# Blocks of 32 slots for every expert of layer 2, four experts to a one-hot product

## The chip, the cores and the metric

The kernel is one launch on one core of a Trainium2 chip. The metric is the device time of that launch in microseconds (us), as the median of several runs. Beside it stands one profiled execution, whose trace gives the busy time and the waits of each engine: PE (TensorE, with its weight loads as PEld), DVE (VectorE), ACT (ScalarE), POOL (GpSimd) and SP (SyncE, which here only issues DMAs).

## The reference, cut to what matters

Two layers run one after the other. Each ends with a grouped mixture of 16 experts, of which a token uses two (in layer 2 only the 256 latent tokens are left, so 512 pairs of token and expert):

```python
best = jnp.argmax(group_score, axis=-1)              # 1 of 4 groups
_, local = lax.top_k(in_group, TOP_K)                # 2 of its 4 experts
w = ROUTED_SCALE * w / jnp.sum(w, axis=-1, keepdims=True)
...
def expert(acc, ew):
    wg, wu, wd, cw = ew                              # 1024x512, 1024x512, 512x1024, one weight per token
    y = (jax.nn.silu(h @ wg) * (h @ wu)) @ wd
    return acc + cw[:, None] * y, None
...
x_lat = layer_norm(alpha * x_lat + g2 * f_lat, ln2_g[l], ln2_b[l])
```

On the inputs that the reference draws, its router sends to the experts of layer 2, in the order in which the kernel takes them, 37, 31, 10, 27, 68, 41, 14, 18, 82, 41, 14, 21, 19, 39, 30 and 20 tokens. Two of these counts are over 64, and six are over 32.

## The kernel before, in words

The order of the instructions on each engine is written out by hand. In a layer's expert stage the tokens are first gathered by expert into the columns of `XgT` (a product with a one-hot matrix). `ORDER` then names the experts one by one; below, expert q is the one at place q of that order, from 0 to 15. An expert's tokens are worked on in blocks of slots. `blocks` lists the first slot and the number of slots of each. The first block always runs. Each further one stands in a nest of branches (`over`), taken by PE, ACT, DVE and POOL where the expert's count of tokens is larger than the block's first slot; a branch hint is given one step ahead (`foretell`). In layer 2 the blocks were 64 slots, then 32, 32, 64 and 64.

For one block the steps are these.

- `take` (DVE) copies the block's columns from `XgT` into a small tile, `xs` for a first block and `xo` for a further one. The place of the columns is read from a register; an expert that is not the first of its group needs two copies (L1510, L1512).
- `up` (PE, L1533) multiplies the block with the two weight matrices `wg` and `wu`. The block's columns are the stationary operand and the weights stream past it. With 64 slots two products of 512 streamed columns stand side by side in the array for each of the eight parts of the contraction; with 32 slots four products of 256 do.
- `gate` (ACT L1539, DVE L1540) makes the hidden values, `turn` (PE L1547, ACT L1548) transposes them.
- `down` (PE, L1564) multiplies them with `wd`, by the same rule of two or four products side by side, into one PSUM tile, `yp`, that all blocks of layer 2 use in turn.
- DVE takes the result out of PSUM, scaled (L1578), in as many pieces as there are products side by side: into `y` for a first block, into `yo` (named `x` in the rows) for a further one.
- `place_rows` (DVE, L1474 and L1475) makes a one-hot matrix with the routing weights, `S` for first blocks and `So` for further ones, and `scatter` (PE, L1481) adds S-transposed times the outputs to four PSUM tiles `cps`, which hold all 256 tokens and the residual until the end of the layer.

With first blocks of 64 slots, two experts fill the 128 rows of one `y` and one `S`, so that `scatter` runs once for two experts. A further block has a scatter of its own, over its 32 rows alone.

The loop over q interleaves neighbours: three eighths of the `up` of expert q+1, `turn` of q, then (in turn with q) `place_rows` or `scatter` of a pair, then the branch with `down` of q and the further blocks of q, then the other five eighths of `up` of q+1 and its `gate`. The expert weights come in pages of 1 MB, six to an expert, 96 in all, through 16 buffers (`feed`): SP issues the load of a page when the page 16 places ahead of it has been read for the last time, further blocks included.

Of the kernel before, what the change touches and what calls it, by code (L numbers as in the profile page):

```python
# [30 lines left out]
ALU = mybir.AluOpType  # L31
# [64 lines left out]
def _body(ctx, tc, nc, I, out, dbg):  # L96
# [6 lines left out]
    pe, act, dve, pool, sp = nc.tensor, nc.scalar, nc.vector, nc.gpsimd, nc.sync  # L103
# [222 lines left out]
    for l in range(NL):  # L326
        first = l == 0
# [970 lines left out]
        for a in range(T):  # L1298
            dve.tensor_scalar(oh[:, a, :], io[:, :CAP], pos[:, a:a + 1], None, op0=ALU.is_equal)

        blocks = [(0, 64), (64, 32), (96, 32)]
        blocks += [(128, 32), (160, 32)] + [(r, 64) for r in range(192, CAP, 64)] if first else [(128, 64), (192, 64)]
        NB = len(blocks)
        RR = (CAP - M0) // 64
        n4, p4 = n6.rearrange("p (g k) -> p g k", k=6), p6.rearrange("p (g k) -> p g k", k=6)
# [113 lines left out]
        def slot_cols():  # L1419


            wide = [128, NB, 16]
            sl, pc, fl, u = (sc[:, n, :16 * NB].rearrange("p (b e) -> p b e", e=16) for n in range(4))
            sid = cnt[:, 7, 0:2]
            pool.iota(sid[:, 0:1], pattern=[[0, 1]], base=0, channel_multiplier=1,
                      allow_small_or_imprecise_dtypes=True)
            for b, (r0, _) in enumerate(blocks):
                pool.memset(sl[:, b, :], float(r0))
            dve.tensor_scalar(sid[:, 1:2], sid[:, 0:1], 64.0, -64.0, op0=ALU.is_ge, op1=ALU.mult)
            dve.tensor_tensor(sid[:, 0:1], sid[:, 0:1], sid[:, 1:2], op=ALU.add)  # L1430
            dve.tensor_scalar(sl, sl, sid[:, 0:1], None, op0=ALU.add)

            def each(n):
                return cnt[:, n, None, :].to_broadcast(wide)

            dve.tensor_tensor(cnt[:, 4], cnt[:, 3], cnt[:, 2], op=ALU.subtract)
            dve.tensor_tensor(cnt[:, 4], cnt[:, 4], cnt[:, 1], op=ALU.subtract)
            thr = cnt[:, 5].rearrange("p (g e) -> p g e", e=4)
            dve.memset(thr[:, :, 0], 0.0)
            dve.tensor_copy(thr[:, :, 1], nA[:, :, 1])  # L1440
            dve.tensor_tensor(thr[:, :, 2], nA[:, :, 2], n4[:, :, 4], op=ALU.add)
            dve.memset(thr[:, :, 3], 1.0e6)
            dve.tensor_tensor(u, sl, each(1), op=ALU.is_ge)
            dve.tensor_tensor(u, u, each(4), op=ALU.mult)
            dve.tensor_tensor(pc, sl, each(2), op=ALU.add)
            dve.tensor_tensor(pc, pc, u, op=ALU.add)
            dve.tensor_tensor(u, sl, each(0), op=ALU.is_ge)
            dve.scalar_tensor_tensor(pc, u, 1.0e6, pc, op0=ALU.mult, op1=ALU.add)
            dve.tensor_tensor(fl, each(5), sl, op=ALU.is_gt)

            for n, t in ((0, pc), (1, fl)):
                d = sc[:, 3, 80 + 8 * n:88 + 8 * n].rearrange("p (j g) -> p g j", j=4)
                t4 = t[:, 0].rearrange("p (g j) -> p g j", j=4)
                for h in range(2):
                    dve.tensor_copy(d[64 * h:64 * h + 64], t4[64 * h:64 * h + 64, h::2, :])
            return pc, fl, sc[:, 3, 80:88], sc[:, 3, 88:96]

        def token_rows():

# [8 lines left out]
            act.activation(posrow, yp_[0][:, 0:256], AF.Copy)  # L1468
            act.activation(w0row, yp_[0][:, 256:512], AF.Copy)
            act.activation(wdrow, pt_[0][:, 256:512], AF.Copy)  # L1470

        def place_rows(dst, rows, pcol, fcol):

            dve.scalar_tensor_tensor(dst[rows], wdrow[rows], fcol[rows], w0row[rows], op0=ALU.mult, op1=ALU.add)  # L1474
            dve.scalar_tensor_tensor(dst[rows], posrow[rows], pcol[rows], dst[rows], op0=ALU.is_equal, op1=ALU.mult)  # L1475
# [74 lines left out]
        def down(e, b):  # L1550
# [15 lines left out]
            if not first:  # L1566
                q = ORDER.index(e)
                if b == 0:
                    rows = slice(64 * (q % 2), 64 * (q % 2) + 64)
                    yt = [y_[q // 2 % 2][:, 512 * n:512 * n + 512] for n in range(2)]  # L1570
                else:
                    rows, yt = slice(64, 64 + Mb), yo
                if b:
                    place_rows(So, rows, pcol[:, b, e:e + 1], fcol[:, b, e:e + 1])
                for j in range(ng):
                    n, c = divmod(N * j, 512)
                    part = slice(Mb * j, Mb * j + Mb)
                    dve.tensor_tensor(yt[n][rows, c:c + N], yp[part, :N], g2[n][part, c:c + N], op=ALU.mult)  # L1578
                if b:
                    scatter(So, yo, rows)  # L1580
                return
            for j in range(ng):
                src, dst = yp[Mb * j:Mb * j + Mb, :N], y[:, N * j:N * j + N]
# [87 lines left out]
        for q, e in enumerate(ORDER):  # L1671
# [10 lines left out]
            if q == 2 and not first:  # L1682
                for i in tiles:
                    for n in range(2):
                        pe.matmul(cps[i, n], ident, X[i][n], start=False, stop=False, skip_group_check=True)
            if not first and q % 2:
                place_rows(S_[q // 2 % 2], slice(0, 128), pcols[:, q // 2:q // 2 + 1], fcols[:, q // 2:q // 2 + 1])
            elif not first and q:
                scatter(S_[(q // 2 - 1) % 2], [y_[(q // 2 - 1) % 2][:, 512 * n:512 * n + 512] for n in range(2)],
                        slice(0, 128))  # L1690
            if q == 0 and LATE:
                for un in late[1:] if LATE == 1 else late:
                    un.mm(pt_[1][:, 256:])
# [225 lines left out]
```

## Time and profile before

| what | value |
|---|---|
| median of 3 runs | 1500.34 us (1496.33 to 1503.78) |
| the profiled execution, its own time | 1505.39 us |
| its span in the trace | 1503.7 us |
| PE busy | 1334.2 us, 89% of the span |
| DVE busy | 739.6 us, 49% |
| ACT busy | 449.3 us, 30% |
| mean granted TensorE clock | 0.949 of full |
| read from HBM | 342.63 MB |

A share of the span is a mean over stages. The expert stage of layer 2 runs from about 1218 us to 1493 us of the span, and after it only the last normalization and the stores remain, up to 1503.7 us. Layer 1 comes before it and keeps its blocks. The granted clock is given as a share of full speed: 1.00 is 2.4 GHz and 0.50 is 1.2 GHz.

### The profile page before, as it was taken

How to read it: one execution, taken by the hardware profiler on the slowest of the kernel's cores; microseconds unless marked ns; L12 is line 12 of the kernel's file. 1: busy time of each engine (PE TensorE's matmuls, PEld its weight loads, DVE VectorE, ACT ScalarE, POOL GpSimd, SP SyncE). 2: the span in 40 equal slices, each digit the busy share in tenths (PEclk: the TensorE clock that was granted, in tenths of full speed). 3: DMA queues.
4: the chain of work that ended last, by engine and by line, in shares of the span. 5: the costliest groups of instructions: out<-in, count | busy, mean ns of one | idle time of the engine just before them, and what ended most of it. 6: DMA issues, size and time to landing. Idle time of an engine off the chain costs nothing. (4 is left out here: it accounts for less than half of the span.)

```text
span 1503.7 us, 21798 instructions
## 1 busy us (share of the span) xinstructions
PE 1334.2 (89%) x8147; PEld 843.9 (56%) x8147; DVE 739.6 (49%) x1448; ACT 449.3 (30%) x781; POOL 138.2 (9%) x251
## 2 busy tenths in 40 slices
PE   5999889999999978988988779869998889989976
PEld 4777667777787853323333368546767753333322
DVE  3376774553466671323222456887676762222323
ACT  2437533333241221210111173764434320000000
POOL 0020000000022210000000441100002110000000
PEclk9999999999999988998989889999999999898988
DMA  9494332332353377998897646535535579988891
GB/s 377 172 376 173 135 143 89 114 143 85 112 191 118 131 321 300 418 414 346 330 386 280 214 131 231 192 130 200 219 118 205 180 309 403 371 325 340 353 402 49
DMA packets 56816, 358.15 MB, mean 238 GB/s; under 512 B 7316, under 2 KB 8116, under 8 KB 17920
## 3 DMA queue, kind: packets, MB, share of 16 engines
q1 hardware_dynamic: 46048, 320.83, 54.7%
q0 software_dynamic: 9808, 33.39, 6.6%
q8 instruction: 111, 1.82, 0.5%
q10 hardware_dynamic: 720, 1.06, 0.2%
q14 instruction: 129, 1.06, 0.2%
HBM read 342.63 MB, written 12.62 MB: 236 GB/s over the span
## 5 line engine op out<-in xcount | busy, mean ns | idle before, releaser
L373 PE MATMUL acc<-whi,pg 128*128 128x512 f32 (+1 forms) x424 | 173.6, 409 | 0.0
L374 PE MATMUL acc<-wlo,pg 128*128 128x512 f32 (+1 forms) x424 | 165.7, 391 | 4.6 <-DVE wlo L361 4.3
L375 PE MATMUL acc<-whi,pg 128*128 128x512 f32 (+1 forms) x424 | 164.8, 389 | 0.0
L361 DVE TENSOR_TENSOR wlo<-pg,whi 128x1024 fp32r<-128x1024 f32 x104 | 127.0, 1222 | 71.5 <-ACT whi L360 71.2
L360 ACT ACTIVATE whi<-pg 128x1024 fp32r<-128x1024 f32 x104 | 109.5, 1055 | 83.5 <-PE acc L375 54.8
L1564 PE MATMUL sd<-pg,lnv 128*64 128x512 f32 (+1 forms) x416 | 78.0, 566 | 21.2 <-issue 11.0
L374 PEld LDWEIGHTS acc<-wlo,pg 128*128 128x128 f32 x424 | 80.6, 190 | 24.5 <-DVE wlo L361 8.7
L373 PEld LDWEIGHTS acc<-whi,pg 128*128 128x128 f32 x424 | 80.6, 190 | 21.8 <-issue 5.2
L375 PEld LDWEIGHTS acc<-whi,pg 128*128 128x128 f32 x424 | 80.4, 190 | 15.9
L1564 PE MATMUL sd<-pb,lnv 128*64 128x512 f32 (+1 forms) x416 | 70.7, 543 | 14.8 <-ACT lnv L1548 7.1
L1533 PE MATMUL acc<-pg,xs 128*64 128x512 f32 x256 | 71.4, 655 | 13.8 <-DMA pg<-in_wg 4.3
L1539 ACT ACTIVATE hh<-sd 64x512 f32<-64x512 f32 (+1 forms) x18 | 10.2, 568 | 198.7 <-PE sd L1533 198.7
L1533 PE MATMUL acc<-pb,xs 128*64 128x512 f32 x256 | 64.1, 617 | 3.4 <-DMA pb<-in_wu 2.6
L1585 DVE COPY y<-sd 64x512 f32<-64x512 f32 (+1 forms) x32 | 17.9, 558 | 99.6 <-ACT y L1587 83.1
L1533 PE MATMUL sd<-pg,xs 128*64 128x512 f32 x256 | 61.5, 621 | 1.5 <-issue 1.5
L373 PE MATMUL acc<-whi,yhi 128*128 128x512 f32 x144 | 60.3, 419 | 0.0
L1533 PE MATMUL sd<-pb,xs 128*64 128x512 f32 x256 | 59.9, 610 | 0.0
L718 ACT ACTIVATE P<-sd,sm 128x512 f32<-128x512 f32 (+1 forms) x48 | 29.0, 614 | 103.1 <-DVE sm L711 103.1
L1564 PEld LDWEIGHTS sd<-pg,lnv 128*64 128x64 f32 (+1 forms) x416 | 25.4, 135 | 60.3 <-issue 53.9
L375 PE MATMUL acc<-whi,ylo 128*128 128x512 f32 x144 | 57.0, 396 | 0.8 <-DVE ylo L553 0.8
L374 PE MATMUL acc<-wlo,yhi 128*128 128x512 f32 x144 | 56.9, 395 | 0.0
L1533 PEld LDWEIGHTS acc<-pg,xs 128*64 128x64 f32 x256 | 23.3, 149 | 57.6 <-issue 46.0
(470 smaller groups left out, 2378.4 us busy)
## 6 DMA issues: line engine op xcount, KB each, us to landing
pg<-in_win SPq DMA_DIRECT2D x40, 1024.0 KB, 6.0
pg<-in_wada SPq DMA_DIRECT2D x40, 1024.0 KB, 6.2
pg<-in_wg SPq DMA_DIRECT2D x32, 1024.0 KB, 13.6
pg<-in_wu SPq DMA_DIRECT2D x32, 1024.0 KB, 15.5
pb<-in_wd SPq DMA_DIRECT2D x32, 1024.0 KB, 10.0
pb<-in_wg SPq DMA_DIRECT2D x32, 1024.0 KB, 14.3
pb<-in_wu SPq DMA_DIRECT2D x32, 1024.0 KB, 16.4
pg<-in_wd SPq DMA_DIRECT2D x32, 1024.0 KB, 10.3
```

The lines of the kernel that those rows point to most:

```text
L360: act.activation(hi, raw, AF.Copy)
L361: dve.tensor_tensor(lo, raw, hi.bitcast(F), op=ALU.subtract)
L373: pe.matmul(ps, ah, bh, start=start, stop=False)
L374: pe.matmul(ps, ah, bl, start=False, stop=False)
L375: pe.matmul(ps, al, bh, start=False, stop=stop)
L718: act.activation(p[:, s], bank[g][:, s], AF.Exp, scale=SCALE, bias=sm[:, 0, i:i + 1], accum_out=sm[:, 1, i:i + 1])
L1533: pe.matmul(gu[Mb * j:Mb * j + Mb, :N], xv[:, k, 0:Mb], w[k // 4][:, k % 4, c:c + N], start=k == 0, stop=k == 7, skip_group_check=True)
L1539: act.activation(hh[:, :N], gu[0:64, :N], AF.Silu)
L1564: pe.matmul(yp[Mb * j:Mb * j + Mb, :N], lt, wd[f // 2][:, f % 2, N * j:N * j + N], start=f == 0, stop=f == 3, skip_group_check=True)
L1585: dve.tensor_copy(dst, src)
```

## The change

In layer 2 the list of blocks becomes 32, 32, 32, 32, 64 and 64 slots; in layer 1 the new expression gives the same list as the old one. The outputs of four first blocks now share one `y` tile and one one-hot matrix, so `place_rows` for them comes at q = 3, 7, 11, 15 and `scatter` at q = 4, 8, 12 and after the last expert. The scatter of a further block now runs over all 128 rows: `So` and `yo` are set to zero once (POOL), and for a block of 32 the rows 96 to 128 of `So` are cleared again each time (DVE). The columns that hold each slot's place and choice of weight (`slot_cols`) are made for the new layout.

```diff
-        blocks = [(0, 64), (64, 32), (96, 32)]
-        blocks += [(128, 32), (160, 32)] + [(r, 64) for r in range(192, CAP, 64)] if first else [(128, 64), (192, 64)]
+        if first:
+            blocks = [(0, 64)] + [(r, 32) for r in range(64, 192, 32)] + [(r, 64) for r in range(192, CAP, 64)]
+        else:
+            blocks = [(r, 32) for r in range(0, 128, 32)] + [(r, 64) for r in range(128, CAP, 64)]
...
-            dve.tensor_scalar(sl, sl, sid[:, 0:1], None, op0=ALU.add)
+            dve.tensor_scalar(sl[:, 1:], sl[:, 1:], sid[:, 0:1], None, op0=ALU.add)
+            dve.tensor_scalar(sid[:, 1:2], sid[:, 0:1], 32.0, -32.0, op0=ALU.is_ge, op1=ALU.mult)
+            dve.tensor_scalar(sl[:, 0], sl[:, 0], sid[:, 0:1], sid[:, 1:2], op0=ALU.add, op1=ALU.add)
...
-                d = sc[:, 3, 80 + 8 * n:88 + 8 * n].rearrange("p (j g) -> p g j", j=4)
-                t4 = t[:, 0].rearrange("p (g j) -> p g j", j=4)
-                for h in range(2):
-                    dve.tensor_copy(d[64 * h:64 * h + 64], t4[64 * h:64 * h + 64, h::2, :])
+                for g in range(4):
+                    p = slice(32 * g, 32 * g + 32)
+                    dve.tensor_copy(sc[p, 3, 4 * n:4 * n + 4], t[p, 0, 4 * g:4 * g + 4])
...
+            for t in [So] + yo:
+                pool.memset(t, 0.0)
...
-                    rows = slice(64 * (q % 2), 64 * (q % 2) + 64)
-                    yt = [y_[q // 2 % 2][:, 512 * n:512 * n + 512] for n in range(2)]
+                    rows = slice(32 * (q % 4), 32 * (q % 4) + 32)
+                    yt = [y_[q // 4 % 2][:, 512 * n:512 * n + 512] for n in range(2)]
...
+                    if Mb == 32:
+                        dve.memset(So[96:128], 0.0)
...
-                    scatter(So, yo, rows)
+                    scatter(So, yo, slice(0, 128))
...
-            if not first and q % 2:
-                place_rows(S_[q // 2 % 2], slice(0, 128), pcols[:, q // 2:q // 2 + 1], fcols[:, q // 2:q // 2 + 1])
-            elif not first and q:
-                scatter(S_[(q // 2 - 1) % 2], [y_[(q // 2 - 1) % 2][:, 512 * n:512 * n + 512] for n in range(2)],
-                        slice(0, 128))
+            if not first and q % 4 == 3:
+                k = q // 4
+                place_rows(S_[k % 2], slice(0, 128), pcols[:, k:k + 1], fcols[:, k:k + 1])
+            elif not first and q and q % 4 == 0:
+                k = q // 4 - 1
+                scatter(S_[k % 2], [y_[k % 2][:, 512 * n:512 * n + 512] for n in range(2)], slice(0, 128))
```

On PE, in the loop's step for q = 2 of layer 2, the rows before were these (the last part of `up` of expert 2, `turn`, the residual added to `cps`, the scatter of experts 0 and 1, the branch, and the first rows of the further block):

```order
L1533 MATMUL sd<-pg,xs 64x512 x6
L1547 MATMUL sd<-ident,hh 128x64 x4
L1685 MATMUL acc<-x,ident 128x512 x4
L1481 MATMUL acc<-y,S 128x512 x4
L1611 COMPARE_AND_BRANCH
L1667 REGISTER_ALU
L1907 BRANCH_PREFETCH_HINT
L1533 MATMUL sd<-pb,xo 32x256 x16
L1533 MATMUL sd<-pg,xo 32x256 x16
L1564 MATMUL sd<-pg,lnv 64x512 x8
```

and they are now these:

```order
L1538 MATMUL sd<-pg,xs 32x256 x12
L1552 MATMUL sd<-ident,hh 128x64 x2
L1692 MATMUL acc<-x,ident 128x512 x4
L1618 COMPARE_AND_BRANCH
L1674 REGISTER_ALU
L1915 BRANCH_PREFETCH_HINT
L1538 MATMUL sd<-pb,xo 32x256 x16
L1538 MATMUL sd<-pg,xo 32x256 x16
L1569 MATMUL sd<-pg,lnv 32x256 x16
```

Each product of 64 slots by 512 columns has become two of 32 by 256, the transposes are two in place of four, and no scatter stands at this step any more. The further block keeps its place behind the branch.

On DVE, in the branch of the first further block of expert 0, the rows before were these (the hidden values of the further block, the output of the first block, then the next level of the branch, the one-hot rows and the output of the further block):

```order
L1540 TENSOR_TENSOR hh<-hh,sd 64x256
L1578 TENSOR_TENSOR y<-sd,x 64x512 x2
L1611 COMPARE_AND_BRANCH
L1667 REGISTER_ALU
L1907 BRANCH_PREFETCH_HINT
L1504 TENSOR_LOAD modb
L1504 ISA x2
L1510 ISA
L1510 COPY xo<-XgT 128x8x64
L1540 TENSOR_TENSOR hh<-hh,sd 64x256
L1474 SCALAR_TENSOR_TENSOR So<-moda,sc 32x256
L1475 SCALAR_TENSOR_TENSOR So<-modb,sc,So 32x256
```

and they are now these:

```order
L1545 TENSOR_TENSOR hh<-hh,sd 64x256
L1585 TENSOR_TENSOR y<-sd,x 32x256 x4
L1618 COMPARE_AND_BRANCH
L1674 REGISTER_ALU
L1915 BRANCH_PREFETCH_HINT
L1509 TENSOR_LOAD modb
L1509 ISA x2
L1515 ISA
L1515 COPY xo<-XgT 128x8x32
L1545 TENSOR_TENSOR hh<-hh,sd 64x256
L1580 MEMSET So 32x256
L1479 SCALAR_TENSOR_TENSOR So<-moda,sc 32x256
```

The first block's output leaves PSUM in four pieces of 32 by 256 in place of two of 64 by 512, and the clearing of `So` stands ahead of the one-hot rows.

## Rows read from the trace of the kernel before

**Rows 1.** Windows of the expert stage of layer 2, 20 us each.

```profile
core 0: us, PE busy (x) PEld busy (x) DVE busy (x) ACT busy (x) POOL busy (x), PEclk, DMA share, GB/s
1240.00:1260.00 20.00, 19.42 (x88) 7.64 (x85) 5.51 (x11) 1.95 (x4) 0.00 (x0) 1.00 1.01 419
1300.00:1320.00 20.00, 18.56 (x68) 6.34 (x60) 3.04 (x8) 0.97 (x2) 0.00 (x0) 0.66 0.76 307
1460.00:1480.00 20.00, 18.58 (x80) 6.47 (x78) 4.03 (x7) 0.97 (x2) 0.00 (x0) 0.98 0.40 142
```

**Rows 2.** Timeline of PE, experts 10 and 11: start us, us, instructions, idle before.

```profile
1405.79 3.70 PE L1481 MATMUL acc<-y,S 128*128 128x512 f32 x8
1409.42 3.65 PE L1564 MATMUL sd<-pg,lnv 128*64 128x512 f32 x16
1412.90 4.46 PE L1533 MATMUL sd<-pg,xs 128*64 128x512 f32 x20
...
1420.91 3.65 PE L1564 MATMUL sd<-pb,lnv 128*64 128x512 f32 x16 [0.58 <-issue]
```

**Rows 3.** Timeline of PE, the further block of expert 4.

```profile
1289.92 3.66 PE L1533 MATMUL sd<-pb,xo 128*32 128x256 f32 x64
1293.51 3.65 PE L1564 MATMUL sd<-pb,lnv 128*64 128x512 f32 x16
1297.93 0.31 PE L1547 MATMUL sd<-ident,hh 64*128 64x64 f32 x2 [0.77 <-DVE hh L1540]
1299.35 2.77 PE L1564 MATMUL sd<-pb,lnv 128*32 128x256 f32 x32 [1.11 <-DVE y L1578]
1303.09 7.19 PE L1481 MATMUL acc<-x,So 32*128 32x512 f32 x8 [0.96 <-DVE x L1578]
1310.21 8.93 PE L1533 MATMUL sd<-pg,xs 128*64 128x512 f32 x32
```

**Rows 4.** Timeline of PE, the further block of expert 8.

```profile
1368.13 3.66 PE L1533 MATMUL sd<-pg,xo 128*32 128x256 f32 x64
...
1376.96 1.93 PE L1564 MATMUL sd<-pg,lnv 128*32 128x256 f32 x32 [1.32 <-DVE y L1578]
1379.87 5.01 PE L1481 MATMUL acc<-x,So 32*128 32x512 f32 x8 [0.98 <-DVE x L1578]
1384.81 9.18 PE L1533 MATMUL sd<-pb,xs 128*64 128x512 f32 x32
```

**Rows 5.** Timeline of DVE: slot columns, a further block's gate, the steps of expert 10.

```profile
1225.68 0.70 DVE L1455 COPY sc<-sc 64x8 f32<-64x8 f32 x4
...
1372.27 0.42 DVE L1540 TENSOR_TENSOR hh<-hh,sd 64x256 f32<-64x256 f32 x1 [2.37 <-ACT hh L1539]
...
1403.56 0.69 DVE L1540 TENSOR_TENSOR hh<-hh,sd 64x512 f32<-64x512 f32 x1 [3.43 <-ACT hh L1539]
...
1408.41 0.43 DVE L1512 COPY xs<-XgT  x1 [1.03 <-issue]
1413.20 1.41 DVE L1578 TENSOR_TENSOR y<-sd,x 64x512 f32<-64x512 f32 x2 [4.36 <-PE sd L1564]
```

**Rows 6.** Groups by form, from 1100 us on: xcount, busy us, mean ns, idle before.

```profile
L1578 DVE TENSOR_TENSOR y<-sd,x 64x512 f32<-64x512 f32 x32 | 22.0, 689 | 63.0 <-PE sd L1564 60.1 <-issue 2.4
L1578 DVE TENSOR_TENSOR x<-sd,x 32x256 f32<-32x256 f32 x8 | 3.4, 422 | 3.2 <-PE sd L1564 3.1
```

**Rows 7.** Windows of 2 us, columns as in rows 1.

```profile
1302.00:1304.00 2.00, 1.03 (x5) 0.50 (x2) 1.69 (x4) 0.00 (x0) 0.00 (x0) 0.50 1.03 430
1316.00:1318.00 2.00, 2.00 (x12) 0.67 (x10) 0.69 (x1) 0.59 (x1) 0.00 (x0) 1.00 0.15 61
1384.00:1386.00 2.00, 2.00 (x6) 0.53 (x6) 0.00 (x0) 0.00 (x0) 0.00 (x0) 0.50 1.05 442
```

**Rows 8.** Waits of SP's DMA queue from 1150 us on: us, times, longest.

```profile
SPq L1284 <- PE sd L1564: 132.5, 22, 14.6
```

**Rows 9.** Timeline of DVE, expert 13: a copy that starts late.

```profile
1437.64 0.29 DVE L1512 COPY xo<-XgT  x1 [7.06 <-issue]
```

More of the change, by code (lines that the diff above doesn't have):

```diff
@@ L1451, in slot_cols @@
             for n, t in ((0, pc), (1, fl)):
-                d = sc[:, 3, 80 + 8 * n:88 + 8 * n].rearrange("p (j g) -> p g j", j=4)
-                t4 = t[:, 0].rearrange("p (g j) -> p g j", j=4)
-                for h in range(2):
-                    dve.tensor_copy(d[64 * h:64 * h + 64], t4[64 * h:64 * h + 64, h::2, :])
-            return pc, fl, sc[:, 3, 80:88], sc[:, 3, 88:96]
+                for g in range(4):
+                    p = slice(32 * g, 32 * g + 32)
+                    dve.tensor_copy(sc[p, 3, 4 * n:4 * n + 4], t[p, 0, 4 * g:4 * g + 4])
+            return pc, fl, sc[:, 3, 0:4], sc[:, 3, 4:8]
         def token_rows():
```

## The prediction

> **What bounds the kernel now.** Layer 1 is left as it is, so I read only the expert stage of layer 2, in windows first. PE is busy for 18.6 to 19.4 of 20 us, and the DMA engines are nearly full too where pages are due (share 1.01, 419 GB/s), less where a further block ran (0.76) and near the end (0.40) [rows 1]. So two things run side by side, and the stage follows whichever is late: PE's chain from expert to expert, and the weights. The queue's own waits say how they are tied: SP waited 132.5 us in 22 waits for a `down` to let a page go [rows 8]. PE is the one that is late most of the time, and the end shows it: between 1460 and 1480 us the weights are nearly all there (142 GB/s) while PE still works [rows 1].
>
> PE's timeline gives the size of a step. From the `down` of expert 10 to that of expert 11 it is 1420.91 - 1409.42 = 11.5 us, of which PE waits for 0.6 us [rows 2]. A pair's scatter takes 1409.42 - 1405.79 = 3.6 us [rows 2]. A further block took, from its `up` to the next expert's work and without the `down` of the first block, which runs anyway (3.5 us, 1409.42 to 1412.90 [rows 2]), 1310.21 - 1289.92 - 3.5 = 16.8 us for expert 4 and 1384.81 - 1368.13 - 3.5 = 13.2 us for expert 8 [rows 3, 4]. These two, 30.0 us together, are the only further blocks that ran.
>
> **The change, term by term.** The counts say how many blocks there will be: two experts go past 64 tokens, six go past 32, and the two large ones need two further blocks each. That makes 8 further blocks in place of 2.
>
> *The steps without a further block.* Four products of 256 columns side by side stream half as long as two of 512. The rows have this form already: `up` of 32 slots took 1293.51 - 1289.92 = 3.6 us [rows 3], against about 6.9 us for 64 (11.5 less `down` 3.5, `turn` and waits 1.1). `down` of 32 slots took 1.9 us [rows 4], against 3.5. PE alone would then need: `turn` 0.3, wait 0.6, `down` 1.9, five eighths of `up` 2.2, then the gate on ACT and DVE, about 1.1 with its handoffs: 6.1 us from gate to gate. DVE now has a chain of its own that is longer. The gate of expert 10 ended at 1403.56 + 0.69 = 1404.25 and its last copy of `take` began at 1408.41, 4.2 us later [rows 5]. With copies of 32 columns (0.29 us as for 32 columns [rows 9], in place of 0.43) they end some 4.3 us after the gate. Then come four pieces out of PSUM at 0.42 us [rows 6], 1.7 us, and the next gate at 0.42 us [rows 5]: 6.5 us with the handoffs. So a step goes from 11.5 to about 6.6 us, 4.9 us less. There are 15 of them, 73.5 us, and 1.7 us from the first expert's `down`.
>
> The Trainium skill says on this, in TensorEngine Tiling (Array Packing), section PSUM Bottleneck, that tiling speeds up TensorE but not the way out of PSUM, which can then become the bottleneck. Rows 5 and 6 agree, since four pieces cost 1.7 us where two of twice the size cost 1.4 us; by PE's time of 6.1 us alone the 15 steps would give 7 us more, and the sum below would be -13 us in place of -6.
>
> *Scatters of first blocks.* Eight become four: 4 x 3.6 = 14.4 us less [rows 2].
>
> *Further blocks.* I walk through a single one. `up` 3.6 us. The `down` of the first block (1.9) is counted above. DVE must finish its copies (4.3 us after the gate) and two more for the next further block, each 1.0 us of issue [rows 5] and 0.29 us, before it can do this block's gate; that ends 7.3 us after the first gate, while `up` ends at 4.6 us. `down` covers 1.9 of these 2.7 us, so PE waits 0.8 us, in the way of the 0.77 us [rows 3]. `turn` 0.3. The further `down` must wait until DVE has cleared the first block's output out of the one tile `yp`; that took 1.3 us before [rows 4] and takes four pieces now: 1.4 us. `down` 1.9, the wait for the first pieces of the output 1.0, the scatter, now on 128 rows as a pair's is, 3.6 [rows 2 to 4]. Sum 12.6 us. Clearing 32 rows of `So` is hidden behind `down`. The clock comes on top: after the waits of the first further block the granted clock was 0.50 (1.2 GHz), and it was 0.50 again after the second one's scatter [rows 7]; the 32-row scatters took 7.2 and 5.0 us for 3.6 us of work at full clock [rows 3, 4]. I expect the drop after the waits to stay and the full-height scatter to end it sooner than the 32-row one did, and add 0.9 us: 13.5 us. The bounds are 11.5 us (full clock throughout, the gate hidden as for expert 8, where it ran at 1372.27, inside the `down` of the first block [rows 5]) and 16.8 us (as for expert 4). Eight at 13.5 us are 108 us, less the 30.0 us of the two now: 78 us more.
>
> *The start.* `slot_cols` stands on DVE ahead of the first gate. Four more small copies (0.70 us for four [rows 5]) and two more small operations, priced like these, add 1.0 us. Clearing `So` and `yo` on POOL is done while DVE and PE work on the first expert, nothing.
>
> *Weights.* A page of 1.05 MB at 419 GB/s [rows 1] takes 2.5 us, an expert 15 us. A step of 6.6 us runs ahead of that, a step with a further block, 20 us, falls behind. Experts 1 to 3, 10 to 12 and 14 to 15 come without one; 16 pages lie ready, 2.7 experts. From expert 10 on PE needs 6 x 6.6 + 13.5 + two scatters 7.2 = 60 us, and the 20 pages that can't yet be in the buffers need 50 us and the last expert's work after them. I take 5 us of waits, bounds 0 and 15 us. Some waits cost nothing twice: while the further blocks of experts 4 and 8 hold their pages the queue stands still, as it did at 1316 us (61 GB/s) [rows 7].
>
> Sum: -75.2 - 14.4 + 78 + 1 + 5 = -5.6 us. The profiled execution's own time, 1505.39 us, would become 1499.8 us. It lies 5 us above the median of the runs, 1500.34 us, so I take the same difference from there: **1495 us**. The change trades two amounts of some 80 to 90 us; the price at which a further block makes it even is (75.2 + 14.4 - 1 - 5 + 30) / 8 = 14.2 us, and the two measured ones lie on either side of it. Half a per cent, 7.5 us, is about what a measurement of this kernel can tell from no change.
>
> **Rivals.** *Cheap blocks.* The two experts with two further blocks overlap the second `up` with the first block's way out of PSUM, and the clock stays up behind the full-height scatters: 11.5 us a block, 16 us less, 1479 us. For it speaks the 13.2 us of expert 8, of which 1.4 us is its slow scatter. Against it, the six new blocks meet a DVE that has no slack left.
>
> *Dear blocks, slower.* The place is the PE queue behind the further `turn`: waits of 0.8, 1.4 and 1.0 us in a row, with little work between. If the clock falls to 0.50 there each time and stays through `down`, scatter and the next `up`, as after expert 4, a block costs 16.8 us: 26 us more, 1521 us. From 14.2 us a block on the kernel does not gain, from 15.1 us it is slower than can be missed. Against it speaks that half of the 16.8 us was the 32-row scatter's doing.
>
> *Late instructions.* A copy on DVE that waited for nothing shown began 7.06 us late, in a stretch with the DMA engines full [rows 9]. Before, 5 us of slack in each step hid such a gap; now DVE is the chain. Two or three that show cost 8 to 15 us more: about 1505 us. The Trainium skill, Runtime: NRT & Kernel Launch, section Instruction fetch mechanics, states that a taken branch to a target outside the fetched pages must fetch it by DMA before work goes on. That would fit row 9, but no row names its cause.
>
> *Weights set the end.* If the last pages land no earlier than now, PE's gain is waited away: 15 us of waits, about 1505 us.
>
> **How the numbers follow.** About even, with a price near 13.5 us (1486 to 1504 us): 0.42. Cheap blocks: 0.25. Dear blocks: 0.18. Late instructions or weights: 0.15. Of the first case I put 0.15 below 1492.8 us, 0.23 within, 0.04 above 1507.8 us; cheap blocks are all faster; dear blocks 0.02 within and 0.16 slower; the last case 0.08 within and 0.07 slower. That gives faster 0.40, same 0.33, slower 0.27. The range leaves out the dearest and cheapest tenth: 1475 to 1515 us.
>
> **What would show it.** Right: two steps without a further block 6 to 7 us apart from `down` to `down` where pages are ready; eight further blocks with scatters on 128 rows; each 12 to 15 us; PE waits for pages in the last third. Wrong: a price per block outside 11.5 to 16.8 us; steps that stay above 8 us, which would put DVE's copies or late instructions in the place of PE; or an end of the weights' transfers that does not move.

## The result

| kernel | median | range of the runs |
|---|---|---|
| before | 1501.56 us | 1496.33 to 1504.98, 8 runs |
| after | 1511.32 us | 1509.40 to 1516.02, 8 runs |

The ratio is 1.0074, 95% interval 1.0054 to 1.0093: the changed kernel is 9.8 us slower. That lies inside the predicted range, but the time moved the other way: 1495 us was predicted, some 5 us less than before.

The two traces start the expert stage of layer 2 some 4 us apart, so the stage is measured inside each trace, from the first `turn` to the end of the last scatter. It took 1493.59 - 1227.16 = 266.4 us before and 1498.89 - 1223.22 = 275.7 us after: the stage holds the whole loss, 9.3 us.

The windows of after that answer to [rows 1], columns as there:

```profile
1240.00:1260.00 20.00, 13.86 (x166) 7.07 (x169) 2.92 (x9) 0.66 (x2) 0.00 (x0) 0.83 0.76 302
1300.00:1320.00 20.00, 16.54 (x166) 7.41 (x158) 7.18 (x18) 1.56 (x5) 0.00 (x0) 1.00 0.68 270
1460.00:1480.00 20.00, 10.44 (x84) 4.43 (x84) 3.86 (x10) 0.93 (x3) 3.13 (x4) 0.83 0.91 286
```

PE is no longer the engine that is full: 13.9 us of 20 in the first window, where it had 19.4. The DMA engines are not full there either (302 GB/s). So neither of the two things that bounded the stage before, PE's work and the weights, fills the time here. PE's own waits show what does. First the timeline of PE in after, at experts 1, 3, 7 and 10:

```profile
1248.35 0.34 PE L1552 MATMUL sd<-ident,hh 64*128 64x64 f32 x2
1254.83 3.58 PE L1569 MATMUL sd<-pb,lnv 128*32 128x256 f32 x32 [6.14 <-issue]
...
1271.21 0.33 PE L1552 MATMUL sd<-ident,hh 64*128 64x64 f32 x2
1276.07 2.31 PE L1569 MATMUL sd<-pb,lnv 128*32 128x256 f32 x17 [4.53 <-issue]
1281.86 1.50 PE L1569 MATMUL sd<-pb,lnv 128*32 128x256 f32 x12 [3.48 <-issue]
...
1356.86 3.64 PE L1569 MATMUL sd<-pg,lnv 128*32 128x256 f32 x32 [5.99 <-issue]
...
1418.72 0.63 PE L1538 MATMUL sd<-pg,xs 128*32 128x256 f32 x5
1422.20 3.72 PE L1538 MATMUL sd<-pg,xs 128*32 128x256 f32 x34 [2.86 <-issue]
```

Between `turn` and `down`, in the middle of a `down` whose first 17 products had run (expert 3), or in the `up` behind it (expert 10), PE stands still for 3 to 6 us, and "issue" says that the profile shows nothing that it waits for. The place is at or soon behind the branch over the further blocks, which is taken when an expert has none. The waits of PE in the stage of after (us, times, longest) name it as the largest item:

```profile
PE sd L1569 <- issue: 31.6, 9, 6.1
PE acc L1486 <- DVE x L1585: 8.8, 8, 1.1
```

The same row of before:

```profile
PE sd L1564 <- issue: 9.1, 7, 2.9
```

Four of before's seven are of 0.58 us, in front of a `down` that waits for ACT's copy anyway (0.53 us there, by the name of ACT, in a run without branches below). That leaves 6.8 us in three.

The granted clock answers to these waits: it was 0.50 (1.2 GHz) from 1252 to 1258 us, in the wait of expert 1 and behind it, and the `down` there took 3.58 us; the `down` of expert 10, after no wait, took 1.93 us.

The steps, from `turn` to `turn`, add up to the stage exactly (the predicted sums are the prediction's own terms):

| steps | before | after | difference | predicted |
|---|---|---|---|---|
| 9 experts without a further block (1, 2, 3, 6, 7, 10, 11, 12, 14) | 131.6 | 112.7 | -18.9 | 9 x -4.9 - 14.4 = -58.5 |
| 6 experts with further blocks (0, 4, 5, 8, 9, 13) | 123.9 | 155.2 | +31.3 | 6 x -4.9 + 78 - 1.7 = +46.9 |
| expert 15 and the last scatter | 10.9 | 7.8 | -3.1 | 0 |
| waits for weights, in all | | | | +5 |
| stage | 266.4 | 275.7 | +9.3 | -6.6 |

The dear part was cheaper than predicted and the sure part failed: 40 us of the expected gain of the plain steps did not come.

### The profile page after: what moved, and what is told of

Read it like the earlier page. It is cut to its first block, busy times and chain, and to the rows that moved or that the text cites. A ratio compares the mean times of both kernels' runs of the same rounds, so it can differ in the third digit from the quotient of the medians.

```text
span 1509.0 us, 24772 instructions
## 1 busy us (share of the span) xinstructions
PE 1289.6 (85%) x9487; PEld 856.7 (57%) x9487; DVE 758.2 (50%) x1539; ACT 448.1 (30%) x793; POOL 139.4 (9%) x257
## 3 DMA queue, kind: packets, MB, share of 16 engines
q8 instruction: 118, 1.93, 0.5%
## 5 line engine op out<-in xcount | busy, mean ns | idle before, releaser
L361 DVE TENSOR_TENSOR wlo<-pg,whi 128x1024 fp32r<-128x1024 f32 x104 | 127.0, 1222 | 71.4 <-ACT whi L360 71.2
L1569 PE MATMUL sd<-pb,lnv 128*32 128x256 f32 (+1 forms) x608 | 69.3, 500 | 34.4 <-issue 23.8
L1569 PE MATMUL sd<-pg,lnv 128*32 128x256 f32 (+1 forms) x672 | 68.4, 457 | 23.1 <-issue 15.9
L1538 PE MATMUL acc<-pg,xs 128*64 128x512 f32 x256 | 66.8, 617 | 12.3 <-DMA pg<-in_wg 5.0
L1544 ACT ACTIVATE hh<-sd 64x256 f32<-64x256 f32 x24 | 9.0, 377 | 201.6 <-PE sd L1538 201.6
L1592 DVE COPY y<-sd 64x512 f32<-64x512 f32 (+1 forms) x32 | 17.9, 558 | 100.1 <-ACT y L1594 82.1
L1569 PEld LDWEIGHTS sd<-pb,lnv 128*32 128x32 f32 (+1 forms) x608 | 28.4, 132 | 63.6 <-issue 50.6
L1569 PEld LDWEIGHTS sd<-pg,lnv 128*32 128x32 f32 (+1 forms) x672 | 28.6, 122 | 51.7 <-issue 38.7
L1553 ACT ACTIVATE lnv<-sd 128x128 f32<-128x128 f32 (+1 forms) x48 | 15.0, 313 | 129.7 <-PE sd L1552 127.1
```

Of the source, the lines that this page charges most:

```text
L361: dve.tensor_tensor(lo, raw, hi.bitcast(F), op=ALU.subtract)
L1538: pe.matmul(gu[Mb * j:Mb * j + Mb, :N], xv[:, k, 0:Mb], w[k // 4][:, k % 4, c:c + N], start=k == 0, stop=k == 7, skip_group_check=True)
L1544: act.activation(hh[:, :N], gu[0:64, :N], AF.Silu)
L1553: act.activation(hT[:, :w], pt[:, :w], AF.Copy)
L1569: pe.matmul(yp[Mb * j:Mb * j + Mb, :N], lt, wd[f // 2][:, f % 2, N * j:N * j + N], start=f == 0, stop=f == 3, skip_group_check=True)
L1592: dve.tensor_copy(dst, src)
```

## The experiments

Times are medians; before ran beside each group, at 1499.3, 1497.9 and 1497.5 us.

**Is it the branches?** (a_nobranch) The further blocks are settled when the program is written, with the counts of this input (the blocks that run stand in line):

```diff
+            if not first:
+                if [37, 31, 10, 27, 68, 41, 14, 18, 82, 41, 14, 21, 19, 39, 30, 20][ORDER.index(e)] <= blocks[b][0]:
+                    before(True)
+                    return
...
+                up(e, b, range(8))
...
+                gate(e, b)
+                before(False)
+                over(e, b + 1, v, following)
+                return
             with tc.If(v > blocks[b][0], label=f"further_{l}_{ORDER.index(e)}_{b}") as c:
```

> The changed kernel, with the second layer's further blocks settled when the program is written: the 8 blocks that run stand in line, and the comparisons, branches and hints of that layer are gone, with the code of blocks that don't run. It leaves out the decision on the chip. Theory 1, late instructions: the waits of PE in and in front of `down` (the rows marked as issue, some 47 us over 15 steps) are the time until the instructions behind a branch over the further blocks' code are there. Then they vanish, a step without a further block takes 6 to 7 us where its pages are ready, and the stage falls from 275.7 us to 230 to 250 us: 1466 to 1486 us. Theory 2, late weights: PE runs ahead of the pages and the waits are theirs; then they stay where they are, under another name, and the time stays at 1506 to 1516 us. Theory 3, DVE's chain is longer than costed: steps stay near 9 to 10 us, PE waits for DVE or ACT by name, time 1500 to 1511 us.

Measured 1470.2 us, ratio to before 0.981 [0.978, 0.984]: 41 us less than after. The timeline of PE in this kernel at expert 1, whose step took 13.4 us in after:

```profile
1246.08 0.33 PE L1552 MATMUL sd<-ident,hh 64*128 64x64 f32 x2
1246.84 1.93 PE L1569 MATMUL sd<-pb,lnv 128*32 128x256 f32 x32 [0.43 <-ACT lnv L1553]
1248.60 0.61 PE L1538 MATMUL sd<-pb,xs 128*32 128x256 f32 x8
1249.03 3.21 PE L1538 MATMUL sd<-pg,xs 128*32 128x256 f32 x56
1252.16 0.33 PE L1552 MATMUL sd<-ident,hh 64*128 64x64 f32 x2
```

The step is 1252.16 - 1246.08 = 6.1 us; experts 6 and 10 took 6.7 and 6.3. The nine experts without a further block took 82.0 us together, where after took 112.7. So 30.7 of the 40 us that were missing are back. No wait of PE in the stage is marked issue any more. Waits for pages come in their place, 10.5 us in all and all of them in those nine steps, the largest:

```profile
PE sd L1538 <- DMA pg<-in_wu: 5.0, 3, 1.8
PE sd L1538 <- DMA pg<-in_wg: 4.5, 1, 4.5
```

Theory 1 stands. Late weights and DVE's chain are refuted as the main cause: the loads and DVE's work were left as they were, and the steps without a wait for a page, a scatter or the residual's products in them (experts 1, 6, 10 and 14) fell to 6.1 to 7.1 us. The run takes away branches, hints and the code of blocks that don't run all at once; the runs below take these apart.

**The same for the kernel before** (b_nobranch), with the same edit:

> The kernel before with the second layer's further blocks settled when the program is written, as in a_nobranch: two run, the comparisons, branches and hints are gone. It leaves out the decision on the chip. Theory 1, late instructions, hidden before by the longer step: the waits of PE marked as issue sum to 9.6 us before, and the 4.7 us marked DMA in the first `down` after 1451 us may be one of them, so 10 to 16 us go: 1483 to 1490 us, and the change without branches is worth 13 to 20 us (a_nobranch 1470.2). Rival: branches cost both kernels alike, 1460 to 1472 us, and the change's own arithmetic brought nothing.

Measured 1476.7 us, 0.985 [0.982, 0.988]: 21 us less than before, where I expected 10 to 16 and the rival 26 or more; the branches cost after 41 us. The change without branches is worth 6.5 us, less than the 13 to 20 that I expected.

**And with the padding added to that** (b_nobranch_pad), to see what blocks of 32 and groups of four bring by themselves. Padding here means that a further block's scatter runs over 128 rows, of which those that hold no slot are zero:

> The kernel before with the further blocks settled when the program is written, as in b_nobranch (1476.7 us), and with the padding. It leaves out the decision on the chip. Its two scatters took 4.45 and 3.73 us there and the `up` behind the first 8.9 us. Theory of the clock: 1 to 4 us less, 1473 to 1476 us, so that the blocks of 32 and the groups of four alone, without branches, are worth 3 to 6 us (a_nobranch 1470.2 us). Rival: padding gives what it gave with branches, 1460 us, and the blocks of 32 cost 10 us also without branches.

Measured 1470.5 us, 0.981 [0.978, 0.984]. The padding is worth 6.2 us, more than the 1 to 4 that I expected; the blocks of 32 and groups of four are worth nothing: 1470.2 and 1470.5 us are the same within their ranges. So, the branches aside, the change gains what its padding gains. (In b_nobranch the `up` behind the two scatters took 9.72 and 8.78 us, where 7.09 is its time at full clock; the expectation gives 8.9 for the first.) The waits show one reason why the shorter steps gain nothing: PE waits 10.5 us for pages in a_nobranch and for none here.

**The padding alone, with branches** (b_pad).

```diff
+            for t in [So] + yo:
+                pool.memset(t, 0.0)
...
+                    if Mb == 32:
+                        dve.memset(So[96:128], 0.0)
...
-                    scatter(So, yo, rows)
+                    scatter(So, yo, slice(0, 128))
```

> The kernel before with the padding alone: a further block's scatter runs over 128 rows, with `So` and the two output tiles cleared once and 32 rows of `So` cleared for each block. Two further blocks run. Theory of the clock: the two scatters take 3.7 us each at 2.4 GHz in place of 7.2 and 5.0 us, 4.8 us less, and the next `up` runs at the higher level sooner: 1494 to 1498 us beside about 1501 us. Rival: the scatter is off the path or the clock comes back as late as before: 1500 to 1503 us.

Measured 1482.2 us (1477.5 to 1484.1), 0.989 [0.986, 0.992]: 17 us less than before where the two scatters' 4.8 us were counted, and the fastest of the kernels that decide on the chip, 1.1% below before. Its timeline of PE answers to [rows 3]:

```profile
1297.97 3.73 PE L1483 MATMUL acc<-x,So 128*128 128x512 f32 x8 [1.14 <-DVE x L1582]
1301.62 7.09 PE L1535 MATMUL sd<-pg,xs 128*64 128x512 f32 x32
```

The scatter fell from 7.19 to 3.73 us and the `up` behind it from 8.93 to 7.09; at the second one it was 5.01 to 3.73 and 9.18 to 7.09. That is 3.46 + 1.84 + 1.28 + 2.09 = 8.7 us; I had counted the scatters alone. Another 9.9 us are waits like those above: the issue waits of PE in the stage sum to 9.6 us before and 4.4 us here, and the 4.73 us marked DMA at 1451.80 before are gone. The two profiled executions lie further apart than the medians (1505.4 and 1477.5 us; the stage took 266.4 and 242.9 us), so this splits the profiles' difference and not the 17 us. Why the padding shifts those waits, no run here tells.

**The changed kernel without its padding** (a_nopad; the diff above reversed):

> The changed kernel without the padding: a further block's scatter runs over its own 32 or 64 rows, nothing is cleared. Theory of the clock: the 32-row scatter lets the clock fall to 1.2 GHz or stay there, as in the kernel before, where two scatters and the `up` behind each cost 8.7 us more than with padding (7.19 + 8.93 and 5.01 + 9.18 us against 3.73 + 7.09 us each). Eight of them then cost 15 to 35 us: 1526 to 1546 us. Rival: the 17 us that padding gave the kernel before were mostly other waits that shifted; then 1508 to 1520 us.

Measured 1525.5 us, 1.018 [1.015, 1.021]: 14 us more than after, just under the range of the clock's theory and well over its rival's. The timeline of PE at expert 4's second further block:

```profile
1320.26 7.19 PE L1484 MATMUL acc<-x,So 32*128 32x512 f32 x8 [0.99 <-DVE x L1581]
1327.38 5.61 PE L1536 MATMUL sd<-pg,xs 128*32 128x256 f32 x64
```

At 1322 to 1324 us the granted clock there was 0.50. Six of its eight 32-row scatters took 5.0 to 7.2 us. In after, the same scatter over 128 rows took 3.76 us and the `up` behind it 3.66 us, at a clock of 1.00. The eight scatters sum to 43.8 us here and to 29.9 us in after, which is the 14 us.

**How much of it is the length of the jump?** (a_short) The list of blocks ends at 96 (no later block runs with these counts):

```diff
-            blocks = [(r, 32) for r in range(0, 128, 32)] + [(r, 64) for r in range(128, CAP, 64)]
+            blocks = [(r, 32) for r in range(0, 96, 32)]
```

> The changed kernel with a shorter list of blocks in the second layer: 0, 32 and 64 with 32 slots each, and none from 96 on (none of those runs with these counts). Every comparison that decides something stays; what falls is the code that a branch jumps over, on PE from 351 instructions of an expert to 155 (261 in the kernel before). Theory 1, late instructions: a shorter jump lands where instructions are already on the core, so the marked waits fall to less than half, 20 us or more less: 1476 to 1492 us. Theory 2, late weights, and theory 3, DVE's chain: nothing changes, 1506 to 1514 us.

Measured 1502.0 us, 1.002 [1.000, 1.004]: 9 us less than after, less than half of the 20 us or more that I expected from a shorter jump. The waits stay (27.7 us in 8, longest 6.3, in the row that had 31.6). They are not mainly a matter of how far the jump goes.

**Is it the traffic of the weights?** (a_twoexp) All but the first two experts multiply with the pages of those two, and 84 loads are gone:

```diff
+                if not first and n >= 12:
+                    streams[l, nm, e, h] = streams[l, nm, ORDER[n // 6 % 2], h]
+                    fed[0] += 1
+                    continue
```

> The changed kernel, where the second layer loads the pages of its first two experts alone and the others multiply with those again: 84 of 96 transfers of a page are gone. It leaves out the weights of 14 experts. Theory 1, late instructions: PE's waits in and in front of `down` stay, as a jump costs its latency also with the DMA engines idle; they may shrink, since fetches no longer share the engines: of 47 us at least 20 remain, 1480 to 1500 us. Theory 2, late weights: the waits vanish and the steps are 6 to 7 us, 1460 to 1470 us. Theory 3, DVE's chain: steps stay at 9 to 10 us with PE waiting for DVE or ACT by name.

Measured 1479.1 us, 0.987 [0.984, 0.989]: 32 us less than after. The issue waits fall from 31.6 to 15.4 us in 5, so about half needs that traffic. No page was on its way at any of the five, so late weights cannot make them. The longest, 7.42 us behind expert 1's branch, fell together with another load, POOL's four transfers of rows of `lnv`, which run earlier in this kernel; the four with idle engines are of 1.1 to 3.4 us. 15 us remain where I expected 20 or more.

**The hints.** Left out in layer 2 (a_nohint; `foretell` returns at once):

> The changed kernel with the second layer's branch hints left out; every comparison stays. Theory 1a, the hint fetches the instructions behind the branch but comes too late in a short step: without it every branch pays in full, 15 jumps and more with waits of 4 to 7 us in place of 9 with 2.4 to 6.1 us: 1535 to 1580 us. Theory 1b, the hints do little here, the wait is that of the engines' reading on in a stream whose fetches share the DMA engines with the weights: 1505 to 1520 us.

Measured 1538.1 us, 1.027 [1.024, 1.031]: 27 us more than after. The hints do work. All nine plain steps now take 12.2 to 16.9 us. The longest wait is 5.96 us, at expert 7, where after had 5.99 us with the hint: there the hint gained nothing. At expert 1 it is 5.69 us (6.14 with the hint), with a second one of 2.25 us behind it that after does not have.

Given a step earlier, ahead of the branch of the expert before (a_early):

```diff
             v, vn = vn, slots_of(q + 1) if q + 1 < NE else None
+            if q + 1 < NE and not first:
+                foretell(q + 1, vn)
```

> The changed kernel with the hint for the next expert's branch given ahead of the present expert's branch in place of behind it, some 3 to 6 us sooner in a step of 6.6 us. Theory 1a, the hint comes too late: waits shrink, 1480 to 1500 us. Rival: one hint at a time is kept, and the later one takes the place of the one that is about to be used, so that each branch pays in full: 1530 us or more. If neither hint nor its place matters: 1506 to 1516 us.

Measured 1519.9 us, 1.015 [1.011, 1.019]: 8.5 us more than after. "Too late" in the simple sense is refuted, since an earlier hint is worse. It is not as dear as no hint at all, so the rival, that each branch pays in full, is not borne out either.

**More time between hint and branch** (a_twice), by work that is needed for nothing:

```diff
             if q + 1 < NE:
+                if not first:
+                    up(ORDER[q + 1], 0, range(ka, 8))
+                    up(ORDER[q + 1], 0, range(ka))
                 up(ORDER[q + 1], 0, range(ka, 8))
```

> The changed kernel, where `up` of each first block behind the branch is done twice (the second pass overwrites the first): 15 times 32 products of 256 columns, 3.6 us each, 54 us of PE's work that is needed for nothing, between a hint and its branch. Theory 1a, a hint needs more time than a step of 6.6 us gives: steps become 10 us, the waits in and in front of `down` shrink from 37 us to under 15, and the clock stays up; the 54 us cost 20 to 35 us: 1530 to 1546 us. Theory 1b, the waits come of where the code lies or of the number of jumps and not of the time between hint and branch: all waits stay, 1555 to 1570 us.

Measured 1536.2 us, 1.023 [1.018, 1.028]: 54 us of added work cost 25 us, so more than half of it ran where PE would have stood. All issue waits of PE in the stage fell from 37.3 to 20.9 us, not under 15. Time helps, but one wait of 6.2 us (expert 11) is left in a step of 17.9 us.

**Both kernels once more** (after_again, before_again).

> The changed kernel once more, for a second profile. Theory 1, a wait comes of the fetch behind a branch in a short step: the sum of PE's waits marked as issue is 30 to 45 us again, most of them at experts 1, 3 and 7 if the place in the code sets them, at others if it is chance of the traffic. Theory 2 or 3: sums that differ by more than 20 us. Time 1508 to 1516 us.

Measured 1511.5 us. The timeline of PE at expert 1:

```profile
1252.65 0.33 PE L1552 MATMUL sd<-ident,hh 64*128 64x64 f32 x2
1258.80 3.64 PE L1569 MATMUL sd<-pb,lnv 128*32 128x256 f32 x32 [5.82 <-issue]
```

The waits stand at the same experts, most with almost the same lengths: 5.82 at expert 1 (6.14 in the first profile), 3.64 and 2.95 at expert 3 (4.53, 3.48), 2.39 at 6 (2.41), 6.09 at 7 (5.99), 2.89 at 10 (2.86), 4.08 at 13 (4.10). They belong to the program, not to chance. The one at expert 7 is put down to a DMA in one profile and to issue in the other. The waits marked issue sum to 27.8 us, under the 30 to 45 that I expected and 10 us under the first profile's; the one of expert 7, marked DMA here, is most of that.

> The kernel before once more, for a second profile. The 17 us that padding gave hold 8.7 us of slower scatters and `up`s and some 9 us of waits marked as issue. If those waits belong to the kernel, they stand at experts 6, 7 and 13 again, 10 to 16 us in sum; if they are chance of the traffic, they stand elsewhere or sum to 0 to 8 us. The 32-row scatters take 7.2 and 5.0 us again. Time 1494 to 1505 us.

Measured 1501.6 us. The waits of before recur too: 1.92 us at expert 6 (1.89), 1.83 and 3.19 at 7 (1.00, 2.92), 4.59 and 1.66 at 13 (4.73, 1.94). The first 32-row scatter took 7.19 us again, the second 3.75 in place of 5.01.

**What PE waits for, seen in the DMA rows.** The DMA view has a queue of kind instruction that can be counted in any window. These are its rows in after for the 0.25 us from 1251.75, 1273.00, 1279.00 and 1354.00 us (packets, MB, share of 16 engines):

```profile
q8 instruction: 1, 0.02, 26.7%
...
q8 instruction: 1, 0.02, 24.9%
...
q8 instruction: 1, 0.02, 25.5%
...
q8 instruction: 1, 0.02, 24.4%
```

PE went on at 1254.83, 1276.07, 1281.86 and 1356.86 us, 2.9 to 3.1 us behind the start of each window. In windows of 0.25 us over the whole stage, every one of the 13 waits of over 0.7 us that are marked issue, or marked DMA in front of a `down`, ends 2.4 to 3.1 us behind the start of a window with a packet of this queue. Packets come some 7 us apart (39 in 278 us), so this is no coincidence. Two waits that are put down to DVE have the same lag: 1.92 us at 1328.56 (packet at 1325.50) and 2.72 us at 1460.87 (packet at 1458.00). The wait of 2.27 us for a page of `wu` at 1451.08 has not (5.6 us); that one is the weights. So q8 brings PE's instructions, as far as this lag can tell, and PE stands until they come.

The spacing gives the rate. In after seven packets start at 1427.25, 1432.75, 1439.75, 1445.50, 1452.00, 1458.00 and 1463.75 us: 6.1 us apart, with the DMA engines full of weights. Where they are idle (1251.75 and 1255.00 us; in a_twoexp 1411.50, 1414.50 and 1418.00 us) it is 3.0 to 3.5 us. No two packets of after come closer than some 3.2 us (in a_nohint three pairs do, 0.75 to 1.75 us apart), and the four pairs that come that close lie in stretches with a DMA share of 0.07 to 0.34. This is the same row for the stage (1222 to 1500 us) of before, after, b_pad, a_nobranch and b_nobranch:

```profile
q8 instruction: 33, 0.54, 0.8%
```
```profile
q8 instruction: 39, 0.64, 0.9%
```
```profile
q8 instruction: 31, 0.51, 0.7%
```
```profile
q8 instruction: 18, 0.29, 0.4%
```
```profile
q8 instruction: 9, 0.15, 0.2%
```

After needs 39 / 16 = 2.4 packets an expert, before 33 / 16 = 2.1. In after the nine steps without a further block hold 19 packets in 112.7 us, one for each 5.9 us, the spacing found beside the weights. By their number the steps sort themselves: with one packet they took 9.4, 9.7 and 10.3 us, with two 11.2 and 13.5, with three 13.4 to 16.9. Before's nine steps hold 17 packets in 131.6 us, one for each 7.7 us, and most of them hold up nothing.

The last two rows show where more code comes from, branches aside. A first block is 98 products in the timelines in place of 52 (`up` x64, `down` x32, `turn` x2 in place of x32, x16, x4), 736 more for the 16 experts; six more further blocks of 106 products each are 636 more. So somewhat over half of the step from 9 to 18 packets is the narrower products, and the rest is more blocks.

The same count, each over the run's own stage, beside the medians of the runs of the changed kernel that differ in hints or skipped code alone:

| run | q8 packets | median |
|---|---|---|
| a_short (shorter jump) | 36 | 1502.0 us |
| after | 39 | 1511.3 us |
| a_early (hint a step earlier) | 43 | 1519.9 us |
| a_nohint (no hint) | 51 | 1538.1 us |

Each packet more goes with 2 to 3 us more. A hint in its place saves 12 packets, and the earlier hint is worse by 4. a_twoexp, with 38 packets, shows that the number alone is not the price: there they come beside idle DMA engines.

The Trainium skill, Runtime: NRT & Kernel Launch, section Instruction fetch mechanics, states that the instruction memory is refilled in blocks of 16 KiB and that a taken branch out of the pages held forces a fetch before work goes on. These runs agree: 0.64 MB in 39 packets is 16.4 KB each, and the waits vanish with the branches. The Trainium skill says in the same section that the cost of crossing from one block to the next is mostly hidden. The kernels without branches agree: they fetch 9 to 18 packets and no wait of PE in the stage is marked issue.

## Why the prediction was wrong, point by point

**The step that failed** is "So a step goes from 11.5 to about 6.6 us, 4.9 us less". I costed a step by what PE and DVE have to do. That work does take 6.1 to 6.7 us, as a_nobranch shows at experts 1, 6 and 10. (That lies on both sides of PE's 6.1 and DVE's 6.5 us. PE waits for DVE's gate for 0.53 and 0.16 us in the two longer ones and not in the shortest, so the two chains are about equal.) With the branches the nine plain steps took 112.7 us where the prediction has 73, and only expert 2 came near its size (9.4 us, of which 3.6 us are the residual's products that stand in that step). What replaced it is the arrival of PE's instructions: one to three packets a step, 19 in the nine steps, some 6 us apart. The prediction's own sign for this, steps that stay above 8 us, is what the profile showed. The prediction named the mechanism as a rival (*Late instructions*), from one wait of DVE [rows 9], but priced it at two or three waits, 8 to 15 us, and gave it and the weights together 0.15. Branches cost after 41.1 us and before 21.2 us (40 and 22 us by the ratios to before within each group). The difference, 18 to 20 us, is more than the whole error, 15 us, and gives the result its sign.

The warning stood in the same profile. Before has three PE waits marked issue in or in front of a `down`, 1.89 to 2.92 us long, and the wait of 4.73 us marked DMA at 1451.80 has a q8 packet 3.0 us ahead of it:

```profile
1451.80 3.68 PE L1564 MATMUL sd<-pg,lnv 128*64 128x512 f32 x8 [4.73 <-DMA pb<-in_wg]
```

I took the clean step of 11.5 us as the rule and its waits as accidents; they were the first steps at which the rate of fetches showed.

**Scatters of first blocks** were right: four, at 3.70 us.

**Further blocks** were right in their mean, in part by luck. By the same difference, step less 6.6 us and a scatter, the profile of after gives 10.5 us for each of the four of experts 4 and 8, 14.9, 14.4 and 18.5 us for those of experts 5, 9 and 13: 12.8 us on average (expert 0's, in the first step, left out), against 13.5. Without branches (a_nobranch) it is 11.5, the lower bound; the rest are the waits described, so 18.5 us, outside the bounds, is a block of the usual price with 6.8 us of fetch waits. The 10.5 us lie outside too, on the other side. The full-height scatters took 3.71 to 3.76 us at a clock of 1.00, as expected. That the clock would fall in the block's own waits was wrong: it stayed at 1.00 at expert 4. So the 0.9 us added for the clock stand where fetch waits came, and the work itself was costed too high (12.6 us, 11.5 measured).

**The start**: the small copies took 1.37 us for eight, against 0.70 for four [rows 5], as counted.

**Weights**: in after PE waited 2.3 us for a page that can be told from a fetch; where no fetch holds PE back (a_nobranch) 10.5 us, inside the bounds of 0 and 15. They became the next bound only after the branches were gone. (The prediction's list of experts without a further block leaves out 6 and 7; its sum doesn't use the list.) What held the pages back shows in the waits of SP's queue in the stage, which answer to [rows 8] (there 132.5 us in 22, from 1150 us on):

```profile
SPq L1284 <- PE sd L1552: 97.6, 6, 23.0
SPq L1284 <- PE sd L1569: 66.9, 19, 12.0
```

Six waits of up to 23 us stand behind a `turn`, one for each expert with further blocks, whose pages are kept until its last block: six experts hold their pages now, two did before. In one such stretch the DMA engines idle (share 0.03 to 0.05 from 1304 to 1308 us).

**The sum of the change, as measured**: padding 6.2 us gained, blocks of 32 and groups of four 0.3 us, both without branches; the branches' extra price 18 to 20 us lost. Together 11 to 13 us lost, beside 9.8 us in the direct comparison; the medians of one kernel differ by up to 4 us between groups. That the change without branches gains 6.5 us, near the 5.6 us of the predicted sum, is a balance of misses: the steps and the waits for pages cost more than priced, the further blocks less.

**What stays open**: which instructions the packets bring that a hint saves or an early hint adds, and why the padding alone took away part of before's waits. Each wait's place recurs, so it belongs to the program; that it hangs on where the code lies is not shown, since no run here moved the code without changing anything else.

## What to carry to other kernels

Before you shorten a step that ends in a branch, count the instruction packets that fall into it and the time between them: in after no step without a further block that held two packets or more took under 11 us, though the engines needed 6 to 7. Halving the width of the products doubles their instructions, so work saved per step can come back as code to fetch; without branches that cost no wait here. And try the cheap part of a change by itself: here the padding alone was 1.1% faster than before, and the rest of the change took that back and more.

## What the runs showed of the hardware

- Instruction packets of one queue came 6.1 us apart beside a stream of weights at 415 GB/s, and 3.0 to 3.5 us apart with the DMA engines idle; PE went on 2.4 to 3.1 us behind the start of the 0.25 us in which the packet began.
- Waits of this kind are marked issue, but also DMA or DVE, with the same lag behind a packet.
- A branch hint in its place went with 12 packets fewer than no hint and 4 fewer than a hint one step earlier (39, 51 and 43), and with 27 and 8.5 us less time.
- Eight products over 32 rows took 5.0 to 7.2 us in 9 of 12 scatters of before, before_again and a_nopad, and 3.7 to 4.5 us in the other three and in b_nobranch's two. In the second of before, at 1380 to 1386 us, the granted clock fell from 1.00 to 0.50 while PE was busy without a gap. With the other 96 rows zero those of after took 3.7 to 3.8 us (one of after_again, behind a wait of 4.08 us, 5.38), and the next `up` of b_pad gained up to 2 us as well.
